# Four pairs of chunks of the first FFN by seven block products, in a two-layer audio trunk

## The chip, the cores and the metric

The kernel runs on one core of a Trainium2 chip. The time is that of one execution on the device in microseconds (us). TensorE (PE) multiplies matrices, VectorE (DVE), ScalarE (ACT) and GpSimd (POOL) work on tiles, SyncE (SP) issues the transfers. Each has a queue of its own that it works off in the order in which the program was built; semaphores make one wait for another.

## The reference

The input is x of 1024 tokens by 1024 channels, all in float32. The trunk has two layers; the mixer of the first is attention, that of the second a convolution module, and each layer ends with an FFN:

```python
for layer in range(DEPTH):                      # DEPTH = 2
    hn = rms_norm(h, mix_norm[layer])
    if layer % 2 == 0:                          # gated linear attention and stick-breaking attention
        mix = hybrid_mixer(hn, ...)             # ... @ w_out: the output projection
    else:                                       # pointwise + GLU, depthwise 31 taps, LayerNorm, swish, pointwise
        mix = conformer_conv(hn, ...)
    h = h + mix
    h = h + swiglu(rms_norm(h, ffn_norm[layer]), ffn_w_gate[layer], ffn_w_up[layer], ffn_w_down[layer])

def swiglu(h, wg, wu, wd):                      # wg, wu: 1024 x 2816, wd: 2816 x 1024
    return (jax.nn.silu(h @ wg) * (h @ wu)) @ wd
```

## The kernel before, in words

**Products in three parts.** A float32 operand is split in a high and a low part, and a product is three matmuls (`mm3`, L203): high x high, high x low, low x high. So every row of weights is split too: ScalarE rounds it (`wh`, L90), and VectorE or GpSimd subtracts (`wl`, L91; `weight_engine` says which).

**Halves and chunks.** The tokens are two halves of 512, h0 and h1; the residual stands in eight tiles `xres` of 128 tokens. The FFN's 2816 columns are 22 chunks of 128. `ffn_steps` (L237) makes for each chunk `pg` and `pu` in PSUM (8 x 3 matmuls of 512 columns each), the product `a`, and after each group of chunks two down steps (`down`, L209), whose `po` VectorE adds to the residual (`xr`, L229).

**The order of the work.** A stage is a list of steps that `run` (L184) goes through; it loads and splits the weights of one step ahead. `interleave` (L172) puts steps of one list between those of another, and a scheduler sets the final order on each engine from the list. Each stage opens its own pools of SBUF and PSUM, which take over the memory of the ones before.

1. Input projection and attention. The FFN of the first layer for h0, `f0`, needs only the first half of the attention. Its steps, 11 groups of two chunks, stand between the attention units of the second half (`a1`) as filler, and the last 12 steps behind them. A unit of the attention is a chain: `z` on TensorE, ScalarE, a scan and a difference on VectorE (L646, L648), transposes `wt` (L658), their splits, `po` (L676), and `og` (L683), the last read of PSUM.
2. The convolution stage (pools named ps2). It begins with the output projection for h1 (`out_project(1)`), then the norm `c0` and the pointwise products (`pp`) of h0, whose 31 taps per channel run on VectorE (L1123) into `cs`. `f01`, the first FFN for h1 with all 22 chunks, stands beside them as filler. Then follow the layer norm, the second pointwise product, the same for h1 with the second FFN for h0 (`f10`) beside it, and the token sums (`token_sums`, L860).
3. `five_products(1)` (L897). The second layer's FFN treats its chunks in 11 pairs (`NP`, from L28), chunk f with chunk f + 11, by seven block products (a Strassen-like scheme with four blocks of weights and sums of them, `s1` to `s4`, and four blocks of tokens, `t1` to `t4`, and `b22`). Two of the seven products are made beforehand with h0: `f10` keeps the half sums of the first 11 chunks' pg and pu in DRAM (`m1_d`), so `five_products` makes only five for h1. `token_sums` (L860) makes the sums of tokens (`r`, `hl_f`, `t`) from the norm's transposes `pt_f`. `pair_products` adds a product `ps1g` to the kept half (`mg`), adds `ps3g` to that (`vg`, L959), and only then goes on in the same PSUM tile.

Of the kernel before, what the change touches and what calls it, by code (L numbers as in the profile page):

```python
# [8 lines left out]
F32 = mybir.dt.float32  # L9
F32R = mybir.dt.float32r  # L10
# [8 lines left out]
P = 128  # L19
D = 1024  # L20
T = 1024
# [3 lines left out]
DFF = 2816  # L25
NF = DFF // P

NP = NF // 2  # L28
EPS = 1e-6
TAPS = 31  # L30
MASKED = -1e30
# [10 lines left out]
def trunk(ctx, tc, x, mix_norm, ffn_norm, hy_w_in, hy_w_gate2, hy_b_gate, hy_gla_norm,  # L42
# [129 lines left out]
    def interleave(main, filler):  # L172

        res, done = [], 0
        for i, step in enumerate(main):
            res.append(step)
            n = (len(filler) * (i + 1)) // len(main)
            res += filler[done:n]
            done = n
        return res  # L180
# [3 lines left out]
    def run(steps):  # L184
        ready = [s for s in steps if isinstance(s, tuple)]
        got = {}

        def fetch():
            if ready:
                s = ready.pop(0)  # L190
                got[id(s)] = s[0]()

        fetch()
        for s in steps:
            if isinstance(s, tuple):
                w = got.pop(id(s))
                fetch()
                s[1](w)
                marks.append(next(i for i in reversed(nc.cur_bb.bb.instructions) if i.engine == DVE))
            else:  # L200
                s()
# [35 lines left out]
    def ffn_steps(l, h, hT, xt, ps, ft, act, use_silu, groups, keep=None):  # L237

        raws, acts = {}, {}
        joint = [f for g in groups for f in g[0:len(g) - 1:2]]  # L240

        def weights(f):
            if f not in raws:
                n = 2 if f in joint else 1
                pair = {t: load_cols(w[l], P * f, f"{t}{l}{f}{h}", n * P) for t, w in (("g", ffn_w_gate), ("u", ffn_w_up))}
                for c in range(n):
                    raws[f + c] = {t: pair[t][:, :, P * c:P * c + P] for t in pair}
            return [parts(raws[f][t], f"{t}{l}_{f}_{h}") for t in ("g", "u")]

        def chunk(f, ws):  # L250
            nm = f"{l}_{f}_{h}"
            kept = keep is not None and f < NP
            pr = []
            for t, w in zip(("g", "u"), ws):
                pr.append(ps.tile([P, 512], F32, name=f"p{t}{nm}", tag="a"))
                if not kept:
                    for k in range(NK):
                        mm3(pr[-1], w[0][:, k, :], w[1][:, k, :], hT()[0][:, k, :], hT()[1][:, k, :],
                            k == 0, k == NK - 1)
            if kept:  # L260

                for k0 in (0, 4):
                    for t, (pm, w) in enumerate(zip(pr, ws)):
                        for k in range(k0, k0 + 4):
                            mm3(pm, w[0][:, k, :], w[1][:, k, :], hT()[0][:, k, :], hT()[1][:, k, :],
                                k == 0, k == k0 + 3, skip_group_check=True)
                        if k0 == 0:
                            m1 = ft(f"m{t}{nm}")
                            nc.scalar.copy(m1, pm)
                            nc.sync.dma_start(keep[t, f], m1)  # L270
            s = ft(f"s{nm}")
            if use_silu:
                nc.scalar.activation(s, pr[0], AF.Silu)  # L273
                prod = pr[1]
            else:
                sigmoid(s, pr[0])
                nc.vector.tensor_mul(s, s, pr[0])  # L277
                prod = s
            nc.vector.tensor_mul(prod, s, pr[1])
            at = act(f"a{nm}")  # L280
            split(at[:, 0:TH], at[:, TH:T], prod)
            acts[f] = lambda i: (at[:, sub(i)], at[:, TH + P * (i % 4):TH + P * (i % 4) + P])

        steps, late = [], []
        for g in groups:
            for q, c in enumerate(g):
                steps.append((lambda c=c: weights(c), lambda ws, c=c: chunk(c, ws)))
                if q == min(1, len(g) - 1):
                    steps += late
            late = [down(ffn_w_down[l], P * g[0], [lambda c=c: acts[c] for c in g], xt,  # L290
                         range(4 * h, 4 * h + 4), ps, "b", j, f"d{l}_{g[0]}_{h}") for j in range(2)]
        return steps + late
# [37 lines left out]
    k_d = dr("k_d", [4, P, T])  # L330
    v_d = dr("v_d", [4, P, NT, P])
    o_d = dr("o_d", [8, P, T])
    m1_d = dr("m1_d", [2, NP, P, TH])
    xres = [None] * NT

    def load_x(h):
        for i in range(4 * h, 4 * h + 4):
            t = x_tile(f"xr{i}")[:, 0:D]
            nc.sync.dma_start(t, xin[i * P:(i + 1) * P, :])
            xres[i] = t  # L340
# [21 lines left out]
    with ExitStack() as es:  # L362
# [446 lines left out]
        def first(f):  # L809
            def run_first():  # L810
                with tc.high_priority(2000):
# [4 lines left out]
                                  for h in range(2)]  # L816
        w0 = out_project(0, ps, lambda name: bcp.tile([P, T], F32, name=name, tag="bc")[:, 0:512])
        f0 = ffn_steps(0, 0, lambda: hf, xres, ps, ft, act, False,
                       [[f, f + 1] for f in range(0, NF, 2)])
        input_norm(0, input_stats(0))  # L820
        use_ln_exp = lambda: load_set(LN_EXP_SET)
        use_sigmoid = lambda: load_set(SIGMOID_SET)
# [7 lines left out]
        def first_weights():  # L830
# [8 lines left out]
            + a0[14:] + [q[0][1]] + g0[3:] + [v[0][1]] + o0[:2] + [q[1][1]] + o0[2:] + [v[1][1], gkk[1], lx0]  # L839
            + w0[0:1] + [gqq[1]] + w0[1:3] + [use_ln_exp, k[0][1], k[1][1], use_sigmoid] + w0[3:4] + [gv[0][1]]  # L840
            + w0[4:] + [gv[1][1], r[0][1], r[1][1]]
            + a1[:2] + [ffn_in] + interleave(f0[:-12], interleave(a1[2:], g1 + o1)) + f0[-12:])

# [4 lines left out]
    def psum_pools(es, name, banks):  # L850

        pools = {t: es.enter_context(tc.tile_pool(name=f"{name}{t}", bufs=n, space=PSUM)) for t, n in banks}

        class Ps:
            def tile(self, shape, dt, name, tag):
                return pools[tag].tile(shape, dt, name=name, tag=tag)

        return Ps()
# [37 lines left out]

    def five_products(l, blocks, es, order):  # L897

        pools = {}
        for nm, bufs in order:  # L900
            pools[nm] = es.enter_context(tc.tile_pool(name=f"{nm}3{l}", bufs=bufs))
# [27 lines left out]
        def pair_weights(w, t, f):  # L929

            nm = f"{'gu'[t]}{l}{f}"
            raw = raw_p.tile([P, 2, NK, P], F32, name=f"raw_{nm}", tag="raw")
            for e in range(2):
                c0 = P * (NP * e + f)
                nc.sync.dma_start(raw[:, e], w[:, c0:c0 + P].rearrange("(k p) c -> p k c", p=P))
            a1, a2 = raw[:, 0], raw[:, 1]
            u = ft(f"m{nm}")
            nc.sync.dma_start(u, m1_d[t, f])
            s1 = cvp.tile([P, TH], F32, name=f"s1{nm}", tag="tap", bufs=2).rearrange("p (k c) -> p k c", c=P)
            nc.vector.tensor_add(s1, a2[:, k1, :], a2[:, k2, :])  # L940
            nc.vector.tensor_sub(a2[:, k1, :], a2[:, k1, :], a1[:, k1, :])
            nc.vector.tensor_sub(a1[:, k1, :], s1, a1[:, k1, :])
            nc.vector.tensor_sub(a1[:, k2, :], a1[:, k2, :], a1[:, k1, :])
            s24, s3a = parts(a1, f"s24{nm}"), parts(a2, f"s3a{nm}")
            ws1 = ws_p.tile([P, NK, P], F32R, name=f"ws1{nm}", tag="ws")
            split(ws1[:, k1, :], ws1[:, k2, :], s1)
            part = lambda w, k: (w[0][:, k, :], w[1][:, k, :])
            return u, part(s24, k1), part(s3a, k1), (ws1[:, k1, :], ws1[:, k2, :]), part(s24, k2), part(s3a, k2)
# [74 lines left out]
        for f in range(NP):  # L1023
            mats = pair_steps(f)
            steps += mats[:1] + late + mats[1:]
            late = [pair_down(f, (j,), (0, 1)) for j in range(2)]
        return steps, late

    hT = {}

    with ExitStack() as es:
# [12 lines left out]
        def norm(h, gcol, name):  # L1047
            xn = u_pairs(f"xn_{name}")
            xt = xres[4 * h:4 * h + 4]
            return norm_half(xt, xn, norm_stats(xt, xn, name), gcol, ps, ["n"], name, ACT2)  # L1050

        load_x(1)
        run(out_project(1, ps, ft))

        wd = cp.tile([P, NK, 32], F32, name="wd")
        for hh in range(2):
# [115 lines left out]
        def add_bias(h):  # L1172
            bb = act(f"bb{h}").bitcast(F32)
            nc.sync.dma_start(bb, cv_b_pw2[0].partition_broadcast(P))
            for i in range(4 * h, 4 * h + 4):
                nc.gpsimd.tensor_add(xres[i], xres[i], bb)

        def norm_step(h, gcol, name):
            return lambda: hT.update({name: norm(h, gcol, name)})
# [2 lines left out]
        p1 = pw1_steps(1, lambda: hT["c1"])  # L1182
        s0, s1 = [], []
        ln0, ln1 = layer_norm(0, s0), layer_norm(1, s1)
        f01 = ffn_steps(0, 1, lambda: hT["f01"], xres, ps, ft, act, True, [list(range(f, min(f + 4, NF))) for f in range(0, NF, 4)])
        f10 = ffn_steps(1, 0, lambda: hT["f10"], xres, ps, ft, act, True,
                        [[0, 1, 2], [3, 4], [5, 6, 7], [8, 9, 10]], m1_d)
        c0 = conv_steps(0, range(NK))
        c1 = [interleave(conv_steps(1, cs), conv_steps(1, (q,), (q,))) for cs, q in (((0, 2), 1), ((3, 5, 6, 7), 4))]
        q0 = pw2(0, s0)  # L1190
        run([norm_step(0, mixg[1], "c0"), lambda: add_bias(0)] + p0[:2] + [norm_step(1, ffng[0], "f01")]
            + interleave(p0[2:] + f01[:25], c0) + interleave(f01[25:31], ln0) + f01[31:]
            + [norm_step(1, mixg[1], "c1"), lambda: add_bias(1)] + q0[:2] + p1[:2]
            + interleave(p1[2:4] + q0[2:], c1[0])
            + [norm_step(0, ffng[1], "f10")] + interleave(p1[4:] + f10[:9], c1[1])
# [35 lines left out]
```

## Time and profile of the kernel before

| | us |
|---|---|
| median of three runs (2292.77 to 2300.92) | 2298.97 |
| the profiled execution | 2290.71 |
| its span, first to last instruction | 2288.9 |
| PE busy | 2240.6 |
| DVE busy | 1581.4 |
| ACT busy | 956.7 |
| POOL busy | 493.7 |

The granted clock of TensorE was 0.992 of its full 2.4 GHz over the span. Busy times are sums over stages that differ; a busy PE is not a PE at its peak, since matmuls overlap and one of 512 columns has a row of 0.39 us where the next begins 0.23 us later. How to read a row: a timeline has the start, the duration, engine, line, operation, output and inputs; in brackets stands the idle time before it and what ended it.

### The profile page before, as it was taken

The numbers are of one execution on the slowest core, as the hardware profiler recorded it, in microseconds if no ns is written. First come the engines' busy times: TensorE is split into PE (matmuls) and PEld (weight loads), VectorE is DVE, ScalarE is ACT, GpSimd is POOL, SyncE is SP. The second block draws the span as 40 slices with busy tenths as digits, with TensorE's granted clock in tenths as the row PEclk, the third lists the DMA queues.
The fourth block names the chain that finished last, engine by engine and source line by source line (L and its number), as shares of the span: only waits on it lengthen the run. The fifth ranks groups of instructions, "written<-read, shape, count | busy, mean of one in ns | idle before, by whom it ended". The sixth has DMA issues, their size and how long they took to land. (4 is left out here: it accounts for less than half of the span.)

```text
span 2288.9 us, 28010 instructions
## 1 busy us (share of the span) xinstructions
PE 2240.6 (98%) x10602; PEld 1856.1 (81%) x10602; DVE 1581.4 (69%) x2596; ACT 956.7 (42%) x1594; POOL 493.7 (22%) x273
## 2 busy tenths in 40 slices
PE   7999999999999999999999999999999999999999
PEld 6798888788888888888888878878778788888887
DVE  6587764868788755456676634698834877787676
ACT  6475545655565434423222244556344322222221
POOL 0000000000000004444443445778634300000000
PEclk9999999999999999999999999999999999999999
DMA  6254554233432333323323222323332322233222
GB/s 209 93 170 136 177 181 147 81 89 100 131 117 91 119 119 122 109 82 102 101 84 105 80 92 87 107 74 132 126 102 86 113 83 83 65 98 96 65 88 92
DMA packets 221749, 247.98 MB, mean 108 GB/s; under 512 B 9733, under 2 KB 171632, under 8 KB 221614
## 3 DMA queue, kind: packets, MB, share of 16 engines
q1 hardware_dynamic: 221614, 246.19, 33.3%
q8 instruction: 83, 1.36, 0.2%
q14 instruction: 52, 0.43, 0.1%
HBM read 219.42 MB, written 26.74 MB: 108 GB/s over the span
## 5 line engine op out<-in xcount | busy, mean ns | idle before, releaser
L1123 DVE SCALAR_TENSOR_TENSOR cs<-u,wd,cs 128x512 f32<-128x512 f32 x406 | 306.1, 754 | 11.3
L229 DVE TENSOR_TENSOR xr<-xr,po 128x512 f32<-128x512 f32 x232 | 158.3, 683 | 158.0 <-PE po L207 157.2
L91 POOL TENSOR_TENSOR wl_wo<-raw_wo,wh_wo 128x1024 fp32r<-128x1024 f32 x8 | 19.1, 2404 | 882.5 <-ACT wh_wo L90 882.5
L1018 DVE TENSOR_TENSOR xr<-xr,po 128x512 f32<-128x512 f32 x176 | 119.9, 683 | 100.4 <-PE po L207 100.2
L205 PE MATMUL pg<-hh_f,wh_g 128*128 128x512 f32 x440 | 175.6, 399 | 7.1 <-DVE s L277 3.6
L205 PE MATMUL po<-wh_d,a 128*128 128x512 f32 x440 | 173.6, 396 | 2.2 <-DVE xr L229 2.0
L206 PE MATMUL pg<-hl_f,wh_g 128*128 128x512 f32 x440 | 175.1, 398 | 0.0
L207 PE MATMUL pg<-hh_f,wl_g 128*128 128x512 f32 x440 | 174.2, 396 | 0.0
L205 PE MATMUL pu<-hh_f,wh_u 128*128 128x512 f32 x440 | 172.6, 392 | 0.8 <-ACT s L273 0.7
L206 PE MATMUL pu<-hl_f,wh_u 128*128 128x512 f32 x440 | 172.7, 392 | 0.0
L207 PE MATMUL pu<-hh_f,wl_u 128*128 128x512 f32 x440 | 172.5, 392 | 0.0
L206 PE MATMUL po<-wl_d,a 128*128 128x512 f32 x440 | 172.0, 391 | 0.0
L207 PE MATMUL po<-wh_d,a 128*128 128x512 f32 x440 | 171.8, 391 | 0.0
L90 ACT CAST wh_g<-raw_g 128x1024 fp32r<-128x1024 f32 x55 | 57.9, 1053 | 169.0 <-PE po L206 97.9
L91 POOL TENSOR_TENSOR wl_g<-raw_g,wh_g 128x1024 fp32r<-128x1024 f32 x33 | 79.2, 2401 | 156.1 <-ACT wh_g L90 156.1
L205 PEld LDWEIGHTS pg<-hh_f,wh_g 128*128 128x128 f32 x440 | 84.3, 191 | 24.7 <-DVE a L91 3.9
L90 ACT CAST wh_d<-raw_d 128x1024 fp32r<-128x1024 f32 (+1 forms) x58 | 58.4, 1007 | 109.2 <-PE pu L206 61.0
L205 PE MATMUL po<-wh_dp,ap 128*128 128x512 f32 x264 | 102.0, 392 | 2.0 <-DVE xr L1018 0.9
L205 PE MATMUL pp<-hh_c,wh_p 128*128 128x512 f32 x256 | 100.6, 395 | 1.3 <-ACT sg L1091 1.1
L206 PE MATMUL po<-wl_dp,ap 128*128 128x512 f32 x264 | 101.3, 389 | 0.0
L206 PE MATMUL pp<-hl_c,wh_p 128*128 128x512 f32 x256 | 101.1, 395 | 0.0
L207 PE MATMUL po<-wh_dp,ap 128*128 128x512 f32 x264 | 101.0, 389 | 0.0
(442 smaller groups left out, 6038.3 us busy)
## 6 DMA issues: line engine op xcount, KB each, us to landing
raw_g<-in_ffn_w_gate_dram SPq DMA_DIRECT2D x26, 1024.0 KB, 5.2
raw_u<-in_ffn_w_up_dram SPq DMA_DIRECT2D x26, 1024.0 KB, 5.1
raw_p<-in_cv_w_pw_dram SPq DMA_DIRECT2D x16, 1024.0 KB, 5.2
raw_d<-in_ffn_w_down_dram SPq DMA_DIRECT2D x26, 512.0 KB, 3.7
raw_g<-in_ffn_w_gate_dram SPq DMA_DIRECT2D x25, 512.0 KB, 4.9
raw_u<-in_ffn_w_up_dram SPq DMA_DIRECT2D x25, 512.0 KB
raw_dp<-in_ffn_w_down_dram SPq DMA_DIRECT2D x22, 512.0 KB
raw_d<-in_ffn_w_down_dram SPq DMA_DIRECT2D x10, 1024.0 KB, 4.9
```

Of the source, the lines that this page charges most:

```text
L90: nc.scalar.copy(hi, src)
L91: (eng or nc.vector).tensor_sub(lo, src, r32(hi))
L205: nc.tensor.matmul(ps, sh, mh, start=first, stop=False, **kw)
L206: nc.tensor.matmul(ps, sh, ml, start=False, stop=False, **kw)
L207: nc.tensor.matmul(ps, sl, mh, start=False, stop=last, **kw)
L229: nc.vector.tensor_add(xt[i][:, cs], xt[i][:, cs], po)
L1018: nc.vector.tensor_add(xres[i][:, cs], xres[i][:, cs], po)
L1123: i = nc.vector.scalar_tensor_tensor(out, tap, w, acc, op0=ALU.mult, op1=ALU.add)
```

## The change

The first layer's FFN gets the block products too, for four pairs: chunks 0 to 3 with 4 to 7. `NP` becomes one number a layer, `NPS = (4, 11)`. In the attention stage `f0` has seven groups: chunks 0 to 3, whose halves are kept, and 8 to 17; `f0[:-2]` of it is interleaved, and the rest is two steps. Chunks 18 to 21 move to a new stage ("mid") behind the attention, with the output projection for h1 that was in the convolution stage, the first layer's `token_sums(0)`, and the down steps of these chunks behind them. Then `five_products(0)` makes the four pairs for both halves, with the last pair's down steps h0 first. In the convolution stage `f01` keeps only chunks 8 to 21, and its norm is gone from there, as the token sums contain it. `load_x(1)`, `token_sums`, `five_products`, `out_project` and `ffn_steps` are those of before. The diff without the renamed uses of `NP` and `m1_d`:

```diff
-NP = NF // 2
+NPS = (4, NF // 2)
@@ ffn_steps
-            kept = keep is not None and f < NP
+            kept = keep is not None and f < NPS[l]
@@ stage 1
         f0 = ffn_steps(0, 0, lambda: hf, xres, ps, ft, act, False,
-                       [[f, f + 1] for f in range(0, NF, 2)])
+                       [[f, f + 1] for f in (0, 2, 8, 10, 12, 14, 16)], m1_d[0])
-            + a1[:2] + [ffn_in] + interleave(f0[:-12], interleave(a1[2:], g1 + o1)) + f0[-12:])
+            + a1[:2] + [ffn_in] + interleave(f0[:-2], interleave(a1[2:], g1 + o1)) + f0[-2:])
@@ five_products
-            late = [pair_down(f, (j,), (0, 1)) for j in range(2)]
+            if l == 0 and f == NP - 1:
+                late = [pair_down(f, (0, 1), (h,)) for h in range(2)]
+            else:
+                late = [pair_down(f, (j,), (0, 1)) for j in range(2)]
@@ new stage
+    with ExitStack() as mid:
+        weight_engine[0] = nc.vector
+        tp3 = mid.enter_context(tc.tile_pool(name="t3", bufs=1))
+        t3 = tp3.tile([P, 2, 4, TH], F32R, name="t3")
+        with ExitStack() as es:
+            ap = es.enter_context(tc.tile_pool(name="act0", bufs=4))
+            ftp = es.enter_context(tc.tile_pool(name="ft0", bufs=3))
+            xp = es.enter_context(tc.tile_pool(name="xn0", bufs=8))
+            ps = psum_pools(es, "ps0", (("b", 2), ("a", 4), ("n", 2)))
...
+            f0 = ffn_steps(0, 0, lambda: hf, xres, ps, ft, act, True, [[18, 19], [20, 21]])
+            load_x(1)
+            run(f0[:2] + out_project(1, ps, ft) + f0[2:4])
+            xn = [xp.tile([P, 512], F32, name=f"xn_f01{i}", tag="x") for i in range(8)]
+            blocks, hT["f01"] = token_sums(0, hf, ps, ("n", "a"), ft, xn, [[t3[:, m, k, :] for k in range(4)] for m in range(2)])
+            run(f0[4:])
+        with ExitStack() as es:
+            steps, late = five_products(0, blocks, es, (("act", 4), ("s", 4), ("ft", 6)))
+            run(steps + late)
@@ convolution stage
-        load_x(1)
-        run(out_project(1, ps, ft))
-        f01 = ffn_steps(0, 1, lambda: hT["f01"], xres, ps, ft, act, True, [list(range(f, min(f + 4, NF))) for f in range(0, NF, 4)])
+        f01 = ffn_steps(0, 1, lambda: hT["f01"], xres, ps, ft, act, True, [[8, 9, 10, 11], [12, 13, 14, 15], [16, 17, 18, 19], [20, 21]])
-        run([norm_step(0, mixg[1], "c0"), lambda: add_bias(0)] + p0[:2] + [norm_step(1, ffng[0], "f01")]
-            + interleave(p0[2:] + f01[:25], c0) + interleave(f01[25:31], ln0) + f01[31:]
+        run([norm_step(0, mixg[1], "c0"), lambda: add_bias(0)] + f01[:2] + p0[:2]
+            + interleave(p0[2:] + f01[2:16], c0) + interleave(f01[16:20], ln0) + f01[20:]
```

On PE at the end of the attention, before: the products of the last unit (`po`, L676) stand among those of chunk 17 (`pu`), which is one of the eight that follow.

```order
L205 MATMUL pu_17_0_7730<-hh_f_4274,wh_u_17_0_7580 128x512
L206 MATMUL pu_17_0_7730<-hl_f_4275,wh_u_17_0_7580 128x512
L676 MATMUL po_7660<-wth_2_7670,kv_6790 128x256 x2
L207 MATMUL pu_17_0_7730<-hh_f_4274,wl_u_17_0_7581 128x512
L205 MATMUL pu_17_0_7730<-hh_f_4274,wh_u_17_0_7580 128x512
L206 MATMUL pu_17_0_7730<-hl_f_4275,wh_u_17_0_7580 128x512
L676 MATMUL po_7660<-wtl_2_7671,kv_6790 128x256 x2
L676 MATMUL po_7660<-wth_0_7683,kv_6790 128x256 x2
L207 MATMUL pu_17_0_7730<-hh_f_4274,wl_u_17_0_7581 128x512
L205 MATMUL pu_17_0_7730<-hh_f_4274,wh_u_17_0_7580 128x512
L676 MATMUL po_7660<-wtl_0_7684,kv_6790 128x256 x2
L206 MATMUL pu_17_0_7730<-hl_f_4275,wh_u_17_0_7580 128x512
```

After, at the same place: the transposes `pot` of the output norm, the products of the last unit, and the first ones of chunk 18 (`pg_18`) in the new stage.

```order
L789 MATMUL pot_7468<-ident,on_6100 128x128 x4
L676 MATMUL po_7366<-wth_6_7351,kv_6605 128x256
L676 MATMUL po_7366<-wth_6_7351,kv_6605 128x128
L676 MATMUL po_7366<-wtl_6_7352,kv_6605 128x128
L676 MATMUL po_7366<-wtl_6_7352,kv_6605 128x256
L676 MATMUL po_7366<-wth_4_7362,kv_6605 128x256 x2
L676 MATMUL po_7366<-wtl_4_7363,kv_6605 128x256 x2
L676 MATMUL po_7366<-wth_2_7376,kv_6605 128x256 x2
L676 MATMUL po_7366<-wtl_2_7377,kv_6605 128x256 x2
L676 MATMUL po_7366<-wth_0_7389,kv_6605 128x256 x2
L676 MATMUL po_7366<-wtl_0_7390,kv_6605 128x256 x2
L205 MATMUL pg_18_0_7604<-hh_f_4275,wh_g_18_0_7588 128x512
```

The filler that stood between the last unit's matmuls is gone, and a matmul of the new stage follows the last of them.

On DVE at the first layer's norm for h1, before: `hl_f` (L94), the low part of the norm, stands among the convolution's taps (L1121, L1123) and the pointwise product `u`.

```order
L94 SCALAR_TENSOR_TENSOR hl_f_9016<-pt_f_0_9017,vb,hh_f_9015 128x512
L94 SCALAR_TENSOR_TENSOR hl_f_9016<-pt_f_1_9024,vb,hh_f_9015 128x512
L1092 SCALAR_TENSOR_TENSOR u_8916<-pp_8918,vb,sg_8968 128x512
L1121 TENSOR_SCALAR cs_9138<-u_8848,wd,vb 128x512
L94 SCALAR_TENSOR_TENSOR hl_f_9016<-pt_f_2_9031,vb,hh_f_9015 128x512
L94 SCALAR_TENSOR_TENSOR hl_f_9016<-pt_f_3_9038,vb,hh_f_9015 128x512
L1123 SCALAR_TENSOR_TENSOR cs_9138<-u_8848,wd,cs_9138 128x512 x6
L94 SCALAR_TENSOR_TENSOR hl_f_9016<-pt_f_4_9045,vb,hh_f_9015 128x512
L1123 SCALAR_TENSOR_TENSOR cs_9138<-u_8848,wd,cs_9138 128x512
```

After, at the place where the token sums begin: `r` and `pt_f` (L882, L889) are the sums, `hl_f` the low parts, `xr` the additions of the down steps of chunks 18 to 21.

```order
L229 TENSOR_TENSOR xr_3196<-xr_3196,po_1_8385 128x512
L889 TENSOR_TENSOR r_02_8267<-pt_f_2_8255,hl_f_4276 128x512
L882 SCALAR_TENSOR_TENSOR r_03_8294<-pt_f_3_8283,vb,r_03_8293 128x512
L882 SCALAR_TENSOR_TENSOR r_02_8265<-pt_f_6_8260,vb,r_02_8267 128x512
L882 SCALAR_TENSOR_TENSOR hl_f_8155<-pt_f_6_8260,vb,hh_f_8154 128x512
L229 TENSOR_TENSOR xr_3190<-xr_3190,po_0_8399 128x512
L94 SCALAR_TENSOR_TENSOR hl_f_8155<-pt_f_3_8283,vb,hh_f_8154 128x512
L882 SCALAR_TENSOR_TENSOR pt_f_3_8283<-pt_f_3_8283,vb,hh_f_4275 128x512
L229 TENSOR_TENSOR xr_3192<-xr_3192,po_0_8407 128x512
L889 TENSOR_TENSOR r_03_8295<-pt_f_3_8283,hl_f_4276 128x512
```

Every step between two residual additions is now one of the token sums, and the place is no longer inside the convolution.

On DVE at the norm `c0`, after: the additions of the last pair's down steps for h1 (L1019; `xr_7576` to `xr_7582` are its tiles), the copies of the tap weights `wd`, and the norm's first instructions (L132 and on).

```order
L1019 TENSOR_TENSOR xr_7576<-xr_7576,po_1_9740 128x512
L1019 TENSOR_TENSOR xr_7578<-xr_7578,po_1_9748 128x512
L1019 TENSOR_TENSOR xr_7580<-xr_7580,po_1_9756 128x512
L1019 TENSOR_TENSOR xr_7582<-xr_7582,po_1_9764 128x512
L1085 COPY wd<-pwd_9809 128x4x31
L1085 COPY wd<-pwd_9817 128x4x31
L132 TENSOR_TENSOR s_c_9845<-ss_c_9844 128x4
L106 TENSOR_SCALAR nv_c_9856<-s_c_9845 128x4
L107 TENSOR_SCALAR nt_c_9857<-nv_c_9856 128x4
```

Before, the like additions there were those of chunks 20 and 21 for h0, and the output projection's stood behind `s_c`; now h1's additions stand ahead of it.

## Rows read from the trace of the kernel before

**Rows 1.** The page's part 1: busy time of each engine, share of the span, instructions.
```profile
PE 2240.6 (98%) x10602; PEld 1856.1 (81%) x10602; DVE 1581.4 (69%) x2596; ACT 956.7 (42%) x1594; POOL 493.7 (22%) x273
```

**Rows 2.** Stretches of 57 us: busy PE, PEld, DVE, ACT, POOL (instructions), clock, DMA.
```profile
741.00:798.00 57.00, 57.00 (x303) 48.58 (x303) 42.82 (x55) 29.46 (x52) 0.00 (x0) 1.00 0.40 130
1083.00:1140.00 57.00, 57.00 (x254) 47.16 (x253) 38.35 (x54) 15.27 (x18) 24.91 (x11) 1.00 0.27 89
1539.00:1596.00 57.00, 57.00 (x262) 47.11 (x261) 50.31 (x71) 35.60 (x52) 45.62 (x29) 1.00 0.36 121
1596.00:1653.00 57.00, 56.91 (x259) 46.80 (x259) 51.85 (x83) 23.74 (x33) 40.20 (x23) 1.00 0.43 138
```

**Rows 3.** Waits of PE over the span: total, times, longest, in us.
```profile
PE pg L205 <- DVE s L277: 3.6, 1, 3.6
PE ps3g L205 <- DVE vg L959: 3.0, 1, 3.0
PE po L205 <- DVE xr L229: 2.0, 2, 1.5
PE po L205 <- ACT xn_c L130: 0.9, 1, 0.9
```

**Rows 4.** Timeline of DVE at the attention's end: start, duration, line, operation, tiles.
```profile
766.24 2.02 DVE L646 TENSOR_TENSOR_SCAN c<-c 128x896 f32<-128x896 f32 x1 [3.35 <-ACT c L312]
799.75 0.42 DVE L683 TENSOR_TENSOR og<-po,og 64x256 f32<-64x256 f32 x1
```

**Rows 5.** Timeline of PE in the same stretch.
```profile
785.01 1.48 PE L658 MATMUL wt<-ident,b 128*128 128x128 f32 x12
786.24 0.48 PE L206 MATMUL pu<-hl_f,wh_u 128*128 128x512 f32 x1
796.42 0.40 PE L676 MATMUL po<-wtl,kv 128*128 128x256 f32 x2
796.65 0.40 PE L676 MATMUL po<-wth,kv 128*128 128x256 f32 x2
```

**Rows 6.** Timeline of PE at the second layer's token sums.
```profile
1758.43 1.47 PE L878 MATMUL pt_f<-ident,xn_f 128*128 128x128 f32 x12
1809.25 0.79 PE L205 MATMUL ps3g<-hh_f,wh_s24g 128*128 128x512 f32 x1 [2.95 <-DVE vg L959]
```

**Rows 7.** Busy time of the engines in that stretch, columns as in rows 2.
```profile
1761.00:1809.00 48.00, 43.25 (x196) 34.68 (x194) 44.27 (x62) 18.58 (x29) 24.14 (x17) 0.99 0.32 99
```

**Rows 8.** Timeline of DVE in that stretch.
```profile
1761.25 0.75 DVE L882 SCALAR_TENSOR_TENSOR r<-pt_f,vb,r 128x512 f32<-128x512 f32 x1
1761.91 0.75 DVE L882 SCALAR_TENSOR_TENSOR pt_f<-pt_f,vb,hh_f 128x512 f32<-128x512 f32 x1
1778.33 2.85 DVE L940 TENSOR_TENSOR s1g<-raw_g 128x512 f32<-128x512 f32 x1
1791.53 0.68 DVE L940 TENSOR_TENSOR s1u<-raw_u 128x512 f32<-128x512 f32 x1
1808.52 0.68 DVE L959 TENSOR_TENSOR vg<-mg,ps3g 128x512 f32<-128x512 f32 x1
```

**Rows 9.** Timeline of POOL in that stretch.
```profile
1778.24 2.39 POOL L91 TENSOR_TENSOR wl_d<-raw_d,wh_d 128x1024 fp32r<-128x1024 f32 x1
```

**Rows 10.** The norm ahead of those token sums, on DVE and ACT.
```profile
1750.01 0.73 DVE L132 TENSOR_TENSOR s_f<-ss_f 128x4 f32<-128x4 f32 x1 [0.90 <-ACT xn_f L130]
1754.21 1.67 DVE L872 TENSOR_SCALAR xn_f<-xr,rs_f 128x512 f32<-128x512 f32 x4
1754.27 2.56 ACT L872 ACTIVATE xn_f<-xr,rs_f 128x512 f32<-128x512 f32 x4 [2.77 <-DVE rs_f L113]
```

**Rows 11.** The page's part 5: the taps of the convolution.
```profile
L1123 DVE SCALAR_TENSOR_TENSOR cs<-u,wd,cs 128x512 f32<-128x512 f32 x406 | 306.1, 754 | 11.3
```

**Rows 12.** Clock behind the gap at 1809.25, and the first matmul that is fast again.
```profile
1809.00:1813.00 4.00, 3.75 (x9) 2.98 (x10) 4.00 (x6) 2.09 (x4) 3.67 (x2) 0.50 0.77 261
1814.53 0.74 PE L205 MATMUL ps2g<-hh_f,wh_s3ag 128*128 128x512 f32 x1
```

More of the change, by code (lines that the diff above doesn't have):

```diff
@@ L332, in trunk @@
     o_d = dr("o_d", [8, P, T])
-    m1_d = dr("m1_d", [2, NP, P, TH])
+    m1_d = [dr(f"m1_d{l}", [2, NPS[l], P, TH]) for l in range(2)]
     xres = [None] * NT
@@ L897, in five_products @@
     def five_products(l, blocks, es, order):
+        NP = NPS[l]
         pools = {}
@@ L937, in pair_weights @@
             u = ft(f"m{nm}")
-            nc.sync.dma_start(u, m1_d[t, f])
+            nc.sync.dma_start(u, m1_d[l][t, f])
             s1 = cvp.tile([P, TH], F32, name=f"s1{nm}", tag="tap", bufs=2).rearrange("p (k c) -> p k c", c=P)
@@ L1025, in five_products @@
             steps += mats[:1] + late + mats[1:]
-            late = [pair_down(f, (j,), (0, 1)) for j in range(2)]
+            if l == 0 and f == NP - 1:
+                late = [pair_down(f, (0, 1), (h,)) for h in range(2)]
+            else:
+                late = [pair_down(f, (j,), (0, 1)) for j in range(2)]
         return steps, late
     hT = {}
+    with ExitStack() as mid:
[7 more added lines that the diff above has]
+            ps = psum_pools(es, "ps0", (("b", 2), ("a", 4), ("n", 2)))
+            ft = lambda name: ftp.tile([P, 512], F32, name=name, tag="ft")
+            act = lambda name: ap.tile([P, T], F32R, name=name, tag="a")
+            f0 = ffn_steps(0, 0, lambda: hf, xres, ps, ft, act, True, [[18, 19], [20, 21]])
[7 more added lines that the diff above has]
+            run(steps + late)
     with ExitStack() as es:
@@ L1184, in trunk @@
         ln0, ln1 = layer_norm(0, s0), layer_norm(1, s1)
-        f01 = ffn_steps(0, 1, lambda: hT["f01"], xres, ps, ft, act, True, [list(range(f, min(f + 4, NF))) for f in range(0, NF, 4)])
+        f01 = ffn_steps(0, 1, lambda: hT["f01"], xres, ps, ft, act, True, [[8, 9, 10, 11], [12, 13, 14, 15], [16, 17, 18, 19], [20, 21]])
         f10 = ffn_steps(1, 0, lambda: hT["f10"], xres, ps, ft, act, True,
-                        [[0, 1, 2], [3, 4], [5, 6, 7], [8, 9, 10]], m1_d)
+                        [[0, 1, 2], [3, 4], [5, 6, 7], [8, 9, 10]], m1_d[1])
         c0 = conv_steps(0, range(NK))
```

## The prediction

> **What bounds the kernel now.** I read the busy times first: TensorE is busy 2240.6 of 2288.9 us, so all its idle time is 48.3 us, and the next engine, VectorE, stands at 69% [rows 1]. Such a mean says nothing of stages, so the table of stretches came second. In the attention (741 to 798), in the first convolution (1083 to 1140) and in the second one (1539 to 1653) TensorE has no gap, while VectorE is busy 42.82, 38.35, and 50.31 and 51.85 of 57 us [rows 2]: TensorE bounds them all, but what hides VectorE there is FFN matmuls used as filler. Third, the waits of TensorE: the ones that matter here stand where filler is short, 3.6 us at the start of the attention's filler, and 3.0 and 2.0 us at the token sums of the second layer [rows 3].
>
> The change shortens the total of matmuls and takes filler from three places. So it is a sum of one saving and several new gaps.
>
> **The saving.** Once the first chunk of a pair is done for h0 and its halves kept, three products of a chunk with a half are left, of 48 matmuls of 512 columns each for gate and up: 144. Five block products of 12, for gate and for up, are 120: 24 fewer, and 96 for four pairs. The stretch from 1083 to 1140 ran 254 matmuls in 57.00 us without a gap [rows 2], 0.2244 us each (the 390 ns of a single row overlap the next one). 96 x 0.2244 = 21.5 us. Down products and transposes keep their numbers. The wait of 0.9 us of the output projection for a sum of squares of the conv norm [rows 3] goes, since that norm no longer runs beside it.
>
> **The end of the attention.** Before, the last pair of attention units has FFN matmuls between its own to the end, and VectorE's part runs from its first scan at 766.24 to the last read of PSUM, which ends at 800.17: 33.9 us, with 103 filler matmuls on TensorE [rows 4]. After, the first part of the FFN has seven groups in place of eleven and is used up earlier. The order leaves the last three pairs of attention units 125, 78 and 0 filler matmuls where there were 139, 137 and 103, so the last pair has nothing but 63 small matmuls: 12 transposes take 785.01 to 786.24, 0.10 us each, and two of 256 columns 0.23 us [rows 5], so at most 0.13 each, 8.2 us. The first matmul of the new stage stands behind the last read of the attention's PSUM, since it uses its banks. VectorE's 18 instructions from that scan on, of the kinds in this stretch (the first scan 2.02 us, the last read 0.42), sum to 14.2 us without filler's work, some 15.5 with the waits for ScalarE between them. Gap: 15.5 - 8.2 = 7 us. From below 3, if VectorE's first scan is early; from above 33.9 - 8.2 = 25.7, if VectorE takes as long as now. The nearest row is the sum of its own durations, so 7. The pair with 78 filler matmuls: 33.9 - 103 x 0.2244 = 10.8 of its own and 17.5 us of filler make 28.3 us for TensorE, against 42.82/57 x 33.9 = 25.5 us of VectorE. That is 90%, near to where the second convolution stands; 2 us (0 to 8).
>
> **The token sums.** These are new for the first layer; the second has them in the trace, and there TensorE needs 50.8 us from the first transpose (1758.43) to the second half of a product (1809.25), before which it waits for the sum vg [rows 6]. VectorE does 62 instructions in that time, busy 44.27 of 48 us [rows 7], a mean of 0.71 us, and starts 2.8 us after the transposes [rows 6, 8]. TensorE has 45.8 us of work there, 144 down matmuls among it, so its gap is 5.0, which is the two waits of [rows 3]. After, VectorE has 70 instructions from its first one of the token sums to vg (four of them, at L94, keep the third block beside its difference), and TensorE has fewer down matmuls to run meanwhile: 96, with 48 of products and 32 transposes, 144 x 0.2244 + 32 x 0.10 = 35.5 us. 70 x 0.71 + 2.8 = 52.5 us gives a gap of 17.0; at 0.66 us an instruction, the pitch from 1761.25 to 1761.91 [rows 8], it is 49.0 and 13.5. I take 15 (10 to 25). No gap would need 33 us of VectorE, 0.47 us an instruction, and no row of the second layer's has that.
>
> What lies between 0.66 and 0.71 is a collision: s1g took 2.85 us while GpSimd's split of wl_d ran (1778.24, 2.39 us), and its twin s1u 0.68 without one [rows 8, 9]. The Trainium skill ("SBUF — State Buffer", Who interferes with whom) says that a VectorE instruction with two inputs in SBUF contends with a GpSimd instruction that reads SBUF, and that the later one to issue stands still for all of the other. It speaks against this change, in whose stage 12 GpSimd splits of 512 columns run beside VectorE's 20 such instructions: if eight of these were caught for 1.2 us, half of 2.39, the gap would be 25 by that rule. In the trace one of eight such instructions of the first pair was caught in full, which the 0.71 already holds, so the sum goes by the 15.
>
> **The norm before the convolution.** The norm c0 no longer has the output projection beside it. Its first instruction on VectorE stands behind eight additions of the other half. From it the scale takes 1750.01 to 1754.21 and ScalarE four multiplications 2.56 us, in the like norm of the second layer [rows 10]: 6.8 us, and about 2.5 more for what stands between, against 24 matmuls of chunk 9, 5.4 us. 4 us (1 to 8).
>
> **The convolution.** Here f01 gives up 8 of 22 chunks. VectorE's 248 taps at 754 ns are 187 us [rows 11], and 49 others at 0.69 make 34; TensorE has 255 us of work between the first pair of pointwise products and the transposes of the last channel. 87%, where the second convolution ran without a gap at 88 and 91% [rows 2]: 2 us for its ends (0 to 10; a loss of 30 is a rival).
>
> **The clock.** After its gap at 1809.25 TensorE ran at a granted clock of 0.50 (1.2 GHz), and 12 matmuls took until 1814.53: 5.28 us, not 2.69 [rows 6, 12]. So a gap of some microseconds costs 2.6 us more when work returns. Two new ones, at the end of the attention and at the token sums: 5.2 us (0 to 10).
>
> **The steps that cost nothing.** The output projection's loads stand on SP behind its weights, which wait for VectorE; chunks 18 and 19 (96 matmuls, 21.5 us) hide that within about 1 us. The residual's second half (load_x) is loaded while the last group before the stage runs, and is needed only by the output projection's additions. The kept halves add eight copies on ScalarE, eight stores and eight loads on SP, all beside filler matmuls, on an engine that is busy 42% [rows 1]; without that cover each copy would cost its own time, under 1 us. If the cover of the output projection is gone, its wait shows in its first matmul, by 1 to 3 us. The steady pairs of block products run as in the second layer.
>
> **The sum.** -21.5 + 7 + 2 + 15 + 5.2 + 4 + 2 - 0.9 = +12.8 us on the profiled execution's 2290.71, or 2303.5. The median of the runs, 2298.97, lies 8 us above that execution, so on its scale I forecast 2312 us.
>
> **The rivals.**
> *The gaps are all at their low ends* (3 at the attention, 0 for its neighbour, 11 at the token sums, if VectorE needs 0.62 us an instruction, 1 at the norm, 0 in the convolution, 0 of clock): -21.5 + 15 - 0.9 = -7.4, 2291.6. For it: VectorE's sums were made with means, and s1u and vg took 0.68 us, under the mean [rows 8]. Against it: the 5.0 us that the same sum gives for the second layer is what the trace shows.
> *TensorE's work decides and the saving falls whole.* The place is the token sums; it decides if VectorE's work begins early enough, or is short enough, that its chain is done 35.5 us after the first transpose. Then the end of the attention is the only gap and the time is 2299 - 21.5 + 3 = 2280. The Trainium skill ("Perfetto Trace Analysis", Identifying the Most-Contended Engine) would have it so: optimize the engine with the highest occupancy, here TensorE. Its 98% agrees [rows 1]; the waits at the token sums [rows 3] do not.
> *The convolution becomes bound by VectorE.* If the taps wait on each other as at their slowest, 248 at 0.85, and filler's instructions come late, the 34 us that TensorE has over VectorE turn into a loss of about 20 beside the forecast's terms: 2332. For it: the second convolution is at 91%; against it: no gap there.
>
> **How the numbers follow.** A measurement of this kernel tells about 0.5%, 11.5 us, from no change. Forecast 0.46 (spread of its terms from -2 to +27: slower by over 0.5% in 0.27 of it, the same in 0.19); low ends 0.32 (faster 0.10, same 0.22); saving whole 0.14 (faster); convolution bound 0.08 (slower). So faster 0.24, the same 0.41, slower 0.35. The forecast's own range is 2300 to 2326; with the other cases until no more than a tenth is left out at either side it is 2281 to 2330.
>
> **What would show it.** In the profile after: about 96 matmuls fewer; a gap of TensorE of 5 to 10 us before pg of chunk 18, put down to the last og; waits for vg, or for xr before it, of 13 to 17 us in the first layer's token sums, with a granted clock near 0.5 behind them; some 4 us before the transposes of c0; no gap in the convolution. If TensorE waits under 5 us for vg, the forecast is wrong by that, and the second rival holds; if it waits in the convolution for taps (cs), the third.

## The result, and the profile after

The changed kernel takes 2324.36 us (median of six runs, 2322.85 to 2328.35), the one before, run beside it, 2297.93. The ratio is 1.012, with a 95% interval of 1.0105 to 1.0136: slower by 1.2%, some 27 us. Forecast was 2312, slower by 13: the time lies in the forecast's own range, 2300 to 2326, near its upper end, and the slowdown is twice the forecast. The profiled execution took 2328.0 us, its span is 2325.1, 36.2 longer than that of before. The two profiled executions lie some 11 us further apart than the medians, and the tables below are of these two.

The page's first part of the kernel after (busy us, share, instructions):

```profile
PE 2239.0 (96%) x10506; PEld 1844.2 (79%) x10506; DVE 1685.4 (72%) x2752; ACT 966.3 (42%) x1616; POOL 440.8 (19%) x257
```

Against [rows 1] TensorE has 96 matmuls fewer, as was counted, and is busy only 1.6 us less, in part because it ran for some 24 us more at a granted clock of 0.50, where a matmul takes longer. VectorE has 104 us more to do and GpSimd 53 less: block products need sums of weights and tokens, and the splits of f01's first eight chunks, which GpSimd did, are VectorE's now.

Busy time by stage of the kernel after (columns as in [rows 2]): the attention's end, the new stage up to the token sums, these, the rest of the four pairs, and the start of the convolution:

```profile
720.00:772.00 52.00, 43.62 (x232) 36.15 (x231) 44.63 (x58) 25.41 (x49) 0.00 (x0) 0.93 0.31 102
772.00:857.00 85.00, 83.60 (x368) 68.59 (x367) 39.99 (x63) 33.13 (x51) 0.00 (x0) 1.00 0.31 100
857.00:917.00 60.00, 49.92 (x216) 37.50 (x215) 53.61 (x80) 25.61 (x40) 24.14 (x16) 0.97 0.26 83
917.00:1074.00 157.00, 154.97 (x678) 126.12 (x677) 110.57 (x157) 38.67 (x50) 7.52 (x3) 1.00 0.24 76
1074.00:1146.00 72.00, 61.24 (x262) 49.28 (x261) 20.20 (x42) 28.93 (x48) 29.80 (x22) 0.88 0.24 75
```

Three stretches have gaps and a clock under 1.00; before, the attention had neither. To price them with the slow matmuls behind them, I took from each trace the time from every matmul's start to the next and subtracted the median for its columns in the kernel before (0.227 us at 512, 0.120 at 256, 0.108 at 128). What is left is loss. Summed by stretch, in us:

| stretch | before | after | forecast of the difference |
|---|---|---|---|
| end of the attention | 0.7 | 14.8 | 9 + 2.6 of clock |
| token sums of layer 1 | - | 15.2 | 15 + 2.6 of clock |
| the four pairs | - | 3.6 | 0 |
| start of the convolution | 0.1 | 18.0 | 4 |
| output projection | 1.7 | 1.9 | -0.9 |
| token sums of layer 2 | 9.0 | 14.3 | 0 |
| rest of the program | 64.3 | 65.6 | 2 |
| sum | 75.8 | 133.4 | |

That is 57.6 us more loss. The medians of all matmuls sum to 2200.2 us before and 2178.4 after, a saving of 21.8, and 57.6 - 21.8 = 35.8 is the profiled difference to within 0.4.

The waits of TensorE in the three stretches (total, times, longest), the attention's end first:

```profile
PE po L676 <- ACT wth L90: 3.9, 2, 2.5
PE wt L658 <- ACT c L312: 1.5, 2, 1.0
PE po L676 <- DVE og L683: 1.3, 2, 0.8
PE pg L205 <- DVE og L683: 0.9, 1, 0.9
```

At the token sums:

```profile
PE ps3g L205 <- DVE vg L960: 5.1, 1, 5.1
PE po L205 <- DVE xr L229: 4.0, 7, 1.6
```

At the start of the convolution:

```profile
PE pwd L1084 <- DMA wdrow<-in_cv_w_dw_dram: 6.8, 2, 4.7
PE pp L205 <- ACT sg L1114: 2.1, 1, 2.1
PE pp L205 <- ACT hh_c L93: 1.9, 1, 1.9
```

At the first, the wait of chunk 18 (`pg`) for the last `og` stands where it was forecast, but it is 0.9 us; the longest are those of the small matmuls ahead of it, which wait for their rounding on ScalarE (`wth`). The second is the chain of VectorE. The third was not forecast: the transposes of the tap weights wait for a transfer. SyncE issues it, and ScalarE starts the norm's first square, only when the last down product of the stage before (1094.59 to 1094.98) is through:

```profile
1095.01 0.61 SPq L1081 DMA_DIRECT2D wdrow<-in_cv_w_dw_dram  x2
1095.74 0.62 ACT L130 ACTIVATE xn_c<-xr 128x512 f32<-128x512 f32 x1
```

### The profile page after: what moved, and what is told of

It reads as the page before. It is cut to its first block, busy times and chain, and to the rows that moved or that the text cites. A ratio compares the mean times of both kernels' runs of the same rounds, so it can differ in the third digit from the quotient of the medians.

```text
span 2325.1 us, 27996 instructions
## 1 busy us (share of the span) xinstructions
PE 2239.0 (96%) x10506; PEld 1844.2 (79%) x10506; DVE 1685.4 (72%) x2752; ACT 966.3 (42%) x1616; POOL 440.8 (19%) x257
## 5 line engine op out<-in xcount | busy, mean ns | idle before, releaser
L1019 DVE TENSOR_TENSOR xr<-xr,po 128x512 f32<-128x512 f32 x240 | 163.7, 685 | 147.0 <-PE po L207 147.0
L205 PE MATMUL po<-wh_d,a 128*128 128x512 f32 x344 | 138.6, 405 | 10.0 <-DVE xr L229 9.7
L205 PE MATMUL po<-wh_dp,ap 128*128 128x512 f32 x360 | 139.7, 393 | 3.7 <-DVE xr L1019 2.2
L205 PE MATMUL pg<-hh_f,wh_g 128*128 128x512 f32 x344 | 136.2, 396 | 5.5 <-DVE s L277 3.7
L207 PE MATMUL po<-wh_dp,ap 128*128 128x512 f32 x360 | 137.8, 390 | 0.9 <-DVE ap L91 0.9
L206 PE MATMUL po<-wl_dp,ap 128*128 128x512 f32 x360 | 138.4, 390 | 0.0
L205 PE MATMUL pu<-hh_f,wh_u 128*128 128x512 f32 x344 | 136.1, 396 | 0.1
L206 PE MATMUL pg<-hl_f,wh_g 128*128 128x512 f32 x344 | 135.9, 395 | 0.0
L207 PE MATMUL po<-wh_d,a 128*128 128x512 f32 x344 | 135.4, 394 | 0.0
L207 PE MATMUL pu<-hh_f,wl_u 128*128 128x512 f32 x344 | 135.4, 394 | 0.0
L206 PE MATMUL pu<-hl_f,wh_u 128*128 128x512 f32 x344 | 135.4, 394 | 0.0
L207 PE MATMUL pg<-hh_f,wl_g 128*128 128x512 f32 x344 | 134.9, 392 | 0.0
L207 PE MATMUL pp<-hh_c,wl_p 128*128 128x512 f32 x256 | 102.0, 400 | 0.0
```

What stands on the lines that cost most here:

```text
L205: nc.tensor.matmul(ps, sh, mh, start=first, stop=False, **kw)
L206: nc.tensor.matmul(ps, sh, ml, start=False, stop=False, **kw)
L207: nc.tensor.matmul(ps, sl, mh, start=False, stop=last, **kw)
L1019: nc.vector.tensor_add(xres[i][:, cs], xres[i][:, cs], po)
```

## The experiments

All ratios are to the kernel before, with their intervals; the changed kernel's is 1.0120 (1.0105 to 1.0136). The losses by stretch are worked out as above, from the one profiled execution of each kernel. The kernel before was measured again beside each group of runs, with medians from 2293 to 2298 us, so the ratios are compared and not the times.

**The tap rows loaded ahead (wd).**

```diff
+    wdrow = ctx.enter_context(tc.tile_pool(name="wdr", bufs=1)).tile([P, 512], F32, name="wdrow")
+    for hh in range(2):
+        nc.sync.dma_start(wdrow[32 * hh:32 * hh + TAPS, :], cv_w_dw[0, :, 512 * hh:512 * hh + 512])
...
-            wr = ft(f"wdrow{hh}")
-            nc.sync.dma_start(wr[0:TAPS, :], cv_w_dw[0, :, 512 * hh:512 * hh + 512])
```

> The tap weights' rows are loaded ahead of the new stage, into 2 KB of their own, in place of at the start of the convolution stage. Theory A: the gap before their transposes (waits of 4.7 and 2.1 us, and ten matmuls at the lower clock behind, 2 us) goes as a whole: -9 us, about 2315. Theory B: the norm c0 stands right behind it. Its squares on ScalarE end at 1100.7 in the profile whatever the load does, and VectorE's scale (4 us) and ScalarE's multiplications (2.6) follow, so its transposes start at about 1107.5 in place of 1110.6: -3 us, about 2321, and TensorE waits some 7 us before the transposes of c0 in place of before those of the taps.

Measured 1.0106 (1.0087 to 1.0125), 2318.05 us. The loss there fell from 18.0 to 12.9, not to 9, and another wait took the place: chunk 8's bank, which is free only when ScalarE has done `s`.

```profile
PE pu L205 <- ACT s L273: 6.3, 1, 6.3
```

ScalarE's timeline in this kernel (start, duration, line, operation, tiles) tells why `s` was late:

```profile
1094.69 1.04 ACT L90 CAST wh_p<-raw_p 128x1024 fp32r<-128x1024 f32 x1 [4.38 <-PE po L206]
1095.64 0.62 ACT L130 ACTIVATE xn_c<-xr 128x512 f32<-128x512 f32 x1
1100.55 1.05 ACT L273 ACTIVATE s<-pg 128x512 f32<-128x512 f32 x2
```

Eight squares of the norm c0 stand ahead of it, and they begin only when the last down product of the stage before (1094.49) is through. Theory A falls; B has the size, but not the place.

**More cover for the norm (wd_cov).** `f01[:4] + p0[:2]` in place of `f01[:2] + p0[:2]`, and `f01[4:16]` beside the taps.

> As wd, and chunks 10 and 11 of the first FFN for h1 (96 matmuls, 21.5 us) stand ahead of the first pointwise products, so beside the norm c0. Theory B: the gap of the norm goes too, -9 to -13 us against the changed kernel, 2311 to 2315. Theory A: no better than wd. Theory C: the convolution has 34 us more of TensorE's work than of VectorE's, and loses 21.5 of them, so new waits of the layer norm's transposes or for taps come up later and eat up to 10 us: 2318 to 2325.

Measured 1.0137 (1.0115 to 1.016). The waits of the pointwise products (`pp`) for the norm went; that for `s`, 6.3 us, stayed, and the start of the convolution still lost 8.4. The layer norm behind the convolution lost 20.5 us in place of 7.9: theory C, and a larger price than it named. The convolution has no 21 us of TensorE's work to give away.

**Other memory for the norm (xc).** The norm's eight tiles come from the pool `cv2`, whose tiles the block products have left by then:

```diff
-            xn = u_pairs(f"xn_{name}")
+            xn = u_pairs(f"xn_{name}") if name != "c0" else [
+                [cvp.tile([P, 512], F32, name=f"xn_{name}{i}{j}", tag="cv") for j in range(2)] for i in range(4)]
```

> As wd, and the norm c0 before the convolution squares and scales into tiles of a pool that is open throughout, in place of the convolution stage's own. Theory D: the gaps there come from memory. The stage's own tiles and the tap rows lie where the block products' tiles were and come free with the last down product (1094.9 in the profile), so the squares, which could start at 1083, run from 1095.7 and hold up the silu of chunk 8 and the norm behind them. With other memory the 18 us that TensorE loses from 1075 to 1150 fall to 3 to 6: -12 to -15 us against the changed kernel, 2310 to 2313. Theory B (the norm's own chain is too long for its cover): no better than wd, about 2320.

Measured 1.0070 (1.0055 to 1.0086), 2308.1 us, and a loss of 3.1 us at the start of the convolution in place of 18.0. The first square now follows the addition it needs:

```profile
1078.59 0.63 ACT L130 ACTIVATE xn_c<-xr 128x512 f32<-128x512 f32 x1 [6.42 <-DVE xr L1019]
```

and the stretch from 1074 to 1146 has TensorE at

```profile
1074.00:1146.00 72.00, 69.82 (x322) 57.11 (x322) 29.61 (x52) 30.41 (x49) 37.21 (x27) 1.00 0.31 95
```

at the full clock. So 14.9 of the 18.0 us came from memory that is free only when the last matmul of the stage before is through. Theory D holds; by the ratios the gain is some 11 us, just short of its 12 to 15.

**More filler in the attention (att, att1).** Chunks 18 and 19 (att), or chunk 18 alone (att1), go back to the attention stage:

```diff
-                       [[f, f + 1] for f in (0, 2, 8, 10, 12, 14, 16)], m1_d[0])
+                       [[f, f + 1] for f in (0, 2, 8, 10, 12, 14, 16, 18)], m1_d[0])     # att
+                       [[f, f + 1] for f in (0, 2, 8, 10, 12, 14, 16)] + [[18]], m1_d[0])  # att1
```

> Chunks 18 and 19 go back to the attention stage as its eighth group of filler, and the new stage has chunks 20 and 21 alone. Theory: the 15 us that TensorE loses in the last two pairs of attention units are want of filler, so they fall to under 3; the token sums lose 48 down matmuls of cover, so their gap grows by 10.8. Sum -1 to -3 us, about 2322. Rival: the loss at the end of the attention is that of the stage's change (banks and buffers that must come free), it stays, and the token sums lose 10.8: about 2335.

> Chunk 18 alone goes back to the attention stage, 72 matmuls of filler with its down products; 19 stays ahead of the output projection and covers its loads. Theory: the loss of 15 us at the end of the attention falls by 10 to 13, the token sums lose 24 down matmuls of cover, 5.4 us: -5 to -8, about 2318; no wait of the output projection for its splits, where the eighth whole group had 6.9 us. Rival: the loss at the end comes back in some other wait, no change, 2324.

In both the new stage has only the chunks that are left; in att the output projection is its first step. Measured 1.0146 (1.0129 to 1.0164) and 1.0145 (1.0125 to 1.0166): no gain, where both theories forecast one; by the medians some 6 us worse than the changed kernel, which the intervals do not quite separate. With the eighth group the attention itself loses 3.7 us up to its last matmul, so want of filler is the cause there. But the output projection then stands right behind it and waits for the split of the attention's output: 11.2 us with the slow matmuls behind that wait, so that the two together are about the changed kernel's 14.8, as the rival had it. And the token sums, with 48 matmuls less beside them, lose 23.4 us:

```profile
PE po L205 <- ACT oTh L90: 6.9, 1, 6.9
PE ps1g L205 <- issue: 13.0, 1, 13.0
PE ps3g L205 <- DVE vg L960: 2.9, 1, 2.9
```

("issue" is a wait for nothing that the profile names.) With chunk 18 alone the attention's loss is 12.0, and the token sums' 20.5, by 5.3 more as forecast. What h0 has of TensorE's work is one supply, and in these two runs a place lost about what another gained.

**Chunk 21 behind the start of the token sums (tok).** `run(f0[:2] + out_project(1, ps, ft) + f0[2:3])`, and `f0[3:]` behind the sums. The sums write over the first four blocks of h0, so here chunk 21 computes with other values.

> Chunk 21 stands behind the start of the token sums in place of ahead of their norm; 24 of the down matmuls go ahead of them in exchange. Theory: VectorE's 70 instructions (46.9 us) set the time of the token sums, and TensorE's work beside them grows by 24 matmuls: the gap falls by 5.4 us, about 2319, and the clock behind it may stay up (another 2). Rival: the transposes start earlier but VectorE is held by chunk 21's own product and split, and the end does not move: 2324.

Measured 1.0156 (1.0134 to 1.0179), worse than both the theory and the rival; the token sums lose 21.6 us. Chunk 21 reads what the sums write, so its matmuls wait for them. So this run decides nothing on the cover; it shows that this work cannot stand there.

```profile
PE pg L205 <- ACT hh_f L90: 2.1, 1, 2.1
PE pt_f L878 <- DVE hl_f L882: 1.8, 1, 1.8
```

**GpSimd splits the weights of the new stage (pool).** `weight_engine[0] = nc.gpsimd` in its first line.

> GpSimd splits the weights in the new stage in place of VectorE. Theory (VectorE's chain sets the end of the token sums): four splits of 1.14 us leave the chain from the first sum to vg, and two more stood just ahead of it, so TensorE's gaps there fall by 4.6 to 7 us and the clock behind them may stay up; about 2318. Rival (VectorE and GpSimd contend): VectorE's sums, which have two inputs in SBUF, are caught behind GpSimd's splits of 2.4 us, as s1g was for 2.85 us in the second layer; eight of them or so, up to 10 us: 2325 to 2335.

Measured 1.0221 (1.0202 to 1.0239), 2342.83 us: the rival, and worse than its upper end. The token sums lose 20.3 us in place of 15.2 and the four pairs 12.2 in place of 3.6. The attention's end lost 19.7 in place of 14.8, and why is open; 2.8 of it are more matmuls at the lower clock. VectorE in this kernel, at the fourth block's sums, which took 2.49 us for each four in the second layer and in the changed kernel:

```profile
901.70 2.01 DVE L91 TENSOR_TENSOR ws1g<-s1g,ws1g 128x512 fp32r<-128x512 f32 x1 [0.18 <-ACT ws1g L90]
903.63 9.08 DVE L917 TENSOR_TENSOR t<-hh_f,hl_f 128x512 f32<-128x512 f32 x4
912.63 2.49 DVE L921 TENSOR_TENSOR t<-t,t 128x512 f32<-128x512 f32 x4
```

and GpSimd beside it, where a split of this size takes 2.39 us in [rows 9]:

```profile
903.11 2.85 POOL L91 TENSOR_TENSOR wl_s3ag<-raw_g,wh_s3ag 128x1024 fp32r<-128x1024 f32 x1
905.92 2.84 POOL L91 TENSOR_TENSOR wl_s24u<-raw_u,wh_s24u 128x1024 fp32r<-128x1024 f32 x1
908.72 2.84 POOL L91 TENSOR_TENSOR wl_s3au<-raw_u,wh_s3au 128x1024 fp32r<-128x1024 f32 x1
```

Three of the four sums took 2.88 us each, one for each split that ran: the two engines took turns.

**The three together (comb1).** pool, xc and att1.

> The three together: GpSimd splits in the new stage, the norm c0 and the tap rows in other memory, chunk 18 in the attention. If the three losses are separate, -6 - 13 - 5 = -24: about 2300, even with the kernel before. If they share a cover (what one gains another loses): 2308 to 2315.

Measured 1.0128 (1.0108 to 1.0147), 2321.35 us, beyond both forecasts. The three changes of the ratio would add up to 1.0196, so xc's gain is there, and the losses of the other two are in part one loss; which part is open.

**Fewer additions beside the token sums (xc_grp4).** Chunks 18 to 21 as one group: `[[18, 19, 20, 21]]`.

> As xc, and chunks 18 to 21 are one group of four in the new stage: the same 96 down matmuls stand beside the token sums, but VectorE adds 8 products to the residual there in place of 16. Theory (VectorE's chain of 70 instructions sets the gap): 8 of 0.60 us less, so the loss of 15.8 us at the token sums falls by 4.8, to 11, and nothing else changes: -5 against xc, about 2303. Rival (want of TensorE's work sets it, VectorE has slack): no change against xc, 2308.

Measured 1.0029 (1.0016 to 1.0041), 2300.06 us. The loss at the token sums fell from 15.8 to 12.1, by 3.7 of the 4.8 expected; TensorE had the same matmuls there. That VectorE's chain sets this gap is shown. The ratio fell by more, some 9 us: the second layer's token sums, which no edit touched, lost 8.7 us in this profile and 14.3 in xc's (last section), and whether that holds for the medians is open.

**Three pairs, two pairs (xc_np3, best3, best2).** `NPS = (3, NF // 2)` and `(2, NF // 2)`; each pair less gives the attention a chunk more and f01 two. best3 and best2 have the group of four too.

> As xc, with three pairs in place of four: chunks 0 to 2 are kept, and one chunk more, with its down products, stands in the attention as filler (72 matmuls, 16 us). TensorE does 24 matmuls more, +5.4 us. Theory: the loss at the end of the attention, 15.7 us, is want of filler; by the eighth group and chunk 18 it falls by 3 to 11 with that much more. Sum between -6 and +2 against xc: 2302 to 2310. Rival (the saving of matmuls is what counts, gaps stay): +5.4, 2313.

> Three pairs, chunks 18 to 21 as one group, and the other memory for the norm c0 and the tap rows. If the loss at the token sums (less 3.7 to 4.8 by the group) and that at the end of the attention (less by the filler of the third pair's chunk) are separate, 2296, within 0.2% of the kernel before; if they share, 2300 as each has alone.

> As best3 with two pairs: TensorE does 24 matmuls more, +5.4 us, and one more chunk of h0 stands in the attention. Theory: the loss at the end of the attention, 9 us with three pairs, falls to 2 to 5, so the two about cancel: 2294 to 2299. If the loss is as it was with three pairs: 2301.

| | pairs | ratio | loss, attention's end | loss, token sums |
|---|---|---|---|---|
| xc_grp4 | 4 | 1.0029 (1.0016 to 1.0041) | 14.8 | 12.1 |
| xc_np3 | 3 | 1.0025 (1.0015 to 1.0034) | 9.1 | 15.4 |
| best3 | 3 | 1.0007 (0.9996 to 1.0019) | 8.3 | 12.1 |
| best2 | 2 | 1.0008 (0.9997 to 1.0019) | 4.2 | 10.6 |

Each pair that goes costs 5.4 us of matmuls and gives back some 4 to 6.5 at the end of the attention. xc_np3 gained 10 us on xc, more than its forecast of -6 to +2; 5.5 of that is again the second layer's token sums, in the one profile of each. best3 and best2 came out as forecast. They are level with the kernel before, and no version beat it.

## Why the prediction was right in its direction and short in its size

- **The saving** came as worked out: 21.8 us of matmul time against 21.5.
- **The token sums** came out near the forecast: a loss of 15.2 us for 15 and 2.6. Of it 11.7 stand at waits, where the prediction looked for 13 to 17, and 1.5 on seven slow matmuls. VectorE's 70 instructions ran from 862.94 to the end of vg at 909.90:

```profile
862.94 0.74 DVE L882 SCALAR_TENSOR_TENSOR r<-pt_f,vb,r 128x512 f32<-128x512 f32 x1
887.31 1.17 DVE L941 TENSOR_TENSOR s1u<-raw_u 128x512 f32<-128x512 f32 x1
909.21 0.69 DVE L960 TENSOR_TENSOR vg<-mg,ps3g 128x512 f32<-128x512 f32 x1 [0.56 <-POOL hl_f L91]
```

  47.0 us, 0.67 an instruction, near the lower of the two paces of the prediction. One of them, s1u, was caught behind GpSimd, for half a microsecond; xc_grp4 confirms the mechanism. There is some luck in the pace: the 0.71 of [rows 7] is busy time alone, and with VectorE's own waits its 62 instructions there took 48 us, 0.77 each. Here it hardly waited.
- **The end of the attention** was right in place and short by 2.5 us: 14.1 for 9 and 2.6. The last pair of units lost 10.6 for 7 and 2.6, and the pair with 78 filler matmuls 4.1 for 2. VectorE's part of the last pair ran from 753.37 to 770.86, 17.5 us for the 15.5 of the sum: I summed VectorE's instructions and put the waits for ScalarE between them at 1.3 us. The rounding there is in the chain with each transpose, and TensorE's wait for it was 2.5 in the last pair and 1.4 in the one ahead.
- **The norm before the convolution** is the term that was mis-sized: 18 us for 4, 14 of the 23 us by which the profiled difference exceeds the sum. The prediction priced the norm's own chain against its cover and took its start for granted. That its tiles, and those of the tap rows, lie in memory which the stage before holds to its last matmul was not in the sum. Before, the output projection stood ahead of the norm, and TensorE lost 0.1 us there. xc, which moves nothing but tiles and one load, took 14.9 us of the 18 away.
- **The four pairs** were put at nothing and lost 3.6 us, 2.5 of it at waits for `ap` and `xr`.
- **The rivals.** None came. TensorE waited 5.1 us for vg and 4.0 for xr, so the second falls by its own mark, with 5.1 against 5 for vg only just. The convolution did not become bound by VectorE in the changed kernel (7.9 us of loss for 7.0), but wd_cov shows that 87% left it no 21 us of slack, as the third feared.
- **The clock** was put at 5.2 us for two gaps. Behind vg seven matmuls ran at the granted clock of 0.50, 1.5 us, and not the twelve of [rows 12]; at the attention's end it cost 2.8. The start of the convolution, for which nothing was put, had 36 slow matmuls, 5.9 us of its 18. So what a gap cost behind itself varied from place to place.
- **What the forecast missed beside that**, 5.3 us in the second layer's token sums, does not come with the change: wd, wd_cov, tok, pool and comb1 have the change without it (last section).

The sum was right that the gaps outweigh the saving, but the chances drawn from it put no change (0.41) ahead of slower (0.35), and the time lies in the range because the range reached 14 us above the forecast.

## What to carry to other kernels

In this kernel a stage that opens its own pools could not begin before the last matmul of the one before had let go of the memory, though its data were there: at each border, look which first instructions are held by memory, and give just these tiles of a pool that is open throughout. Work that can be a filler is one supply; here a change that saved 22 us of matmuls and needed cover in three new places lost more than it saved, and the number of pairs (four, three, two) moved little once each gap was priced. And when a change moves work from an idle engine to the second busiest, count that engine's instructions in the places where it is late, not over the whole span.

## What the runs showed of the hardware that was not expected

The same instruction of the second layer, in code that no kernel here changed, took 2.84 to 2.88 us in ten of the fourteen traces and 6.51 to 6.52 in four, each time with the same split on GpSimd beginning some 0.1 us ahead of it. In the changed kernel's profile, VectorE, then the four instructions of GpSimd beside it, then TensorE:

```profile
1807.69 6.51 DVE L941 TENSOR_TENSOR s1g<-raw_g 128x512 f32<-128x512 f32 x1
```

```profile
1807.59 2.41 POOL L91 TENSOR_TENSOR wl_d<-raw_d,wh_d 128x1024 fp32r<-128x1024 f32 x1
1809.94 1.28 POOL L91 TENSOR_TENSOR hl_f<-r,hh_f 128x512 fp32r<-128x512 f32 x1
1811.16 1.28 POOL L91 TENSOR_TENSOR wl_d<-raw_d,wh_d 128x512 fp32r<-128x512 f32 x1
1812.38 1.28 POOL L91 TENSOR_TENSOR hl_f<-r,hh_f 128x512 fp32r<-128x512 f32 x1
```

```profile
1814.85 0.79 PE L205 MATMUL po<-wh_d,a 128*128 128x512 f32 x1 [5.14 <-DVE xr L229]
```

and in wd's, as in [rows 8, 9], VectorE and the instruction of GpSimd behind the split:

```profile
1801.18 2.84 DVE L941 TENSOR_TENSOR s1g<-raw_g 128x512 f32<-128x512 f32 x1
1803.42 1.73 POOL L91 TENSOR_TENSOR hl_f<-r,hh_f 128x512 fp32r<-128x512 f32 x1
```

In the short case s1g ends at 1804.02, 0.55 us behind the split, and it is GpSimd's next instruction that is held up: 1.73 us in place of 1.28. In the long case GpSimd's four follow each other without a gap to 1813.66, each at its full speed, and s1g ends 0.54 us behind the last of them: VectorE was passed over three times. What decides between the two is open. The addition `xr` stands behind s1g, and TensorE waits 5.14 us for it. So with the length goes the loss of the second layer's token sums: 8.7 to 10.4 us with the short one (before, wd, wd_cov, tok, pool, comb1, xc_grp4, the last three) and 13.3 to 14.3 with the long one (after, att, att1, xc). That it also varies among executions of one kernel is not shown, as each has one trace.

The Trainium skill ("SBUF — State Buffer", Who interferes with whom) states that the later of two such instructions stands still for all of the other; the 2.85 us agrees, and so do the 9.08 us for four sums in pool, while in the long case VectorE stood still for four in a row. In the changed kernel's token sums the row that I put above this rule was the better guide (a loss of 15.2 us, not 25); in pool, where GpSimd had four splits more there, the rule was.
